# A hybrid decoder step on one core: where lower parts, a triangular substitution, merge weights and weight differences stand in the order of the engines

## The chip, the cores and the metric

The kernel runs on one core of a Trainium2 chip. Its time is the device time of one execution in microseconds (us), as the median of several runs. A profiled execution has a trace beside its time; the durations and waits below come from that one. The core's engines work beside each other, each on its own list of instructions in order: TensorE (PE in the profile, its weight loads PEld), VectorE (DVE), ScalarE (ACT) and GpSimd (POOL). SyncE (SP) issues most DMAs. An instruction whose inputs or output buffer are not ready holds back everything behind it on its engine.

## The reference, cut to what matters

One layer is computed for 1024 prompt tokens with 16 meta tokens ahead of them, and for 8 x 8 sample tokens, 1104 in all, of width 1024, in fp32.

```python
h = h + 0.5 * rms_norm(swiglu(rms_norm(h, g_pre), w_gate, w_up, w_down), g_post)     # 1024 -> 2816 -> 1024
qkv_pre, z, b, a, sq, sk, sv, g_dn, g_swa = split(rms_norm(h, mix_pre) @ w_in)
qkv = silu(causal_conv(qkv_pre))                                # 4 taps
o_dn, state = gated_delta(l2norm(q), l2norm(k), v, sigmoid(b), decay(a))     # chunks of 64; a unit lower
                                                                # triangular system per chunk and head
o_dn = rms_norm(o_dn) * silu(z)                                 # 8 heads, 128 x 128 states
o_sw = sink_softmax(windowed scores, ALiBi, 16 meta keys) @ v   # 8 query heads on 2 key heads
h = h + rms_norm((sigmoid(g_dn) * o_dn + sigmoid(g_swa) * o_sw) @ w_out, mix_post)
h = h + 0.5 * rms_norm(swiglu(rms_norm(h, g_pre2), ...), g_post2)
```

The new states and the windows of keys and values are outputs too.

## The kernel before

Every large product is made of three fp32r products: a value is split into an upper part (`wh`, `xh`: a cast on ScalarE) and a lower part (`wl`, `xl`: the value less its upper part, a subtraction), and upper x upper, upper x lower and lower x upper are summed in PSUM. So each slice of weights costs a DMA into `raw`, a cast and a subtraction before TensorE can use it.

Order: TensorE runs its instructions in the order of the program's text. On the other engines the framework's scheduler orders them by its own estimate of when each is ready; `keep_in_program_order(op)` pins an operation to the place that the text gives it, and `issue_after(ins)` puts what is issued inside behind `ins` on that instruction's engine. The text itself is woven: generators yield after each few matmuls, and `weave((steps, begin, end, count), ...)` mixes them in proportion. `steps_of(g, n)` takes n steps of one generator.

The stages in order, with the names that matter here:

- **First feed-forward** (0 to about 720 us). Gate ("g") and up ("u") products are made by a fast 2 x 2 block scheme of seven products for pairs of blocks of hidden columns. `gate_up` runs the products 1, 2, 6, 5, 7, 4, 3 into the PSUM banks A, B and C; `w_op` makes their weights from four raw quarters, for products 5, 6, 7 and 4 by differences `T` on VectorE (L256, L267), and `w_split` casts them (L281) and takes their lower parts on POOL (L282). After a product VectorE adds the bank into sums: `u2` after 6, `s` after 7 (L354), then the third sum `u3` = `s` + bank C (L357), after which C is free for product 3. `self.order[0]` is the first pair.
- **Mixer, start** (`before`, 730 to 810). While the feed-forward's last tiles pass through post-norm, residual and pre-norm (transposes L580 into one of two PSUM buffers `tr`, read by L626; L627 and L100 scale rows by factors `rp` and `rn`, whose Square is on ScalarE, L81, and whose power is on POOL, L82 and L83), the first projections of `w_in` already run in three rounds: `ba_steps` and the keys of heads 0 and 1. `w_in(col)` casts a slice on ScalarE (L764) and takes its lower part on POOL (L765); slices 8 and 9 are those keys' weights.
- **Keys, triangular systems, window attention** (810 to 1260). `lane_solve(size 64)` inverts the 128 triangular systems on VectorE in 62 steps of two operations, L1062 (`ltmp` = products) and L1064 (`la` += `ltmp`). They are issued by `solving(...)` one step per ten matmul steps of the query projections that run beside the window attention's blocks (32 blocks in four rounds p = 0 to 3 of eight; TensorE's rounds start at 1031.7, 1095.3, 1162.75 and 1230.85). A block: scores `sc` (L1217 on), VectorE adds the mask into `s` (L1220) and takes row maxima (L1189), ScalarE exponentials, transposes `pt`, casts `ptoh` (L1247), lower parts `ptol` (L1248), then `po` (L1257). The solved systems are stored to memory as they are and, by four ScalarE copies (L1094), transposed; the heads read them later. The pool of `la` gives its memory to the heads' convolution buffers in round 3.
- **Heads** (1260 to 1850). For each head `chain` carries the state through eight tiles: `ch` = R b (L1593), copy `xs` on ScalarE (L1595), `ch` = kd xs (L1598), new state S; `normed` makes the factor `f` on POOL (L1548) and `on` on ScalarE (L1549), `emit` transposes it (L1631). Beside it run the next head's projections and `z_gate`, which evaluates a gate piece by piece (`tz`, L1380). For the last head `z_gate` gets `done = mg.load_w`: after each of its three pieces the buffers of that piece of the mixer's input are free and take slices of `w_out`: DMA (L1709), casts in halves (L1712), lower parts on POOL (L1713).
- **Merge** (1835 to 1970). `begin` multiplies the first tile by `w_out` for heads 0 to 6 while the last chain ends, `begin_last` adds head 7 and copies the two banks out (L1765). The next tile's `yl` is split by L1729 and L1730, and TensorE goes on with `dn` (L128).
- **Second feed-forward** (1970 to 2685), as the first.

## Time and profile before

| | |
|---|---|
| median of 3 runs | 2686.57 us (2686.21 to 2691.09) |
| the profiled execution | 2687.11 us |
| its span, first to last instruction | 2685.2 us |
| mean granted TensorE clock | 0.991 |
| TensorE busy | 2604.9 us of the span |
| VectorE, ScalarE, POOL busy | 1556.6, 1127.4 and 1290.1 us |

The median describes the kernel; the profiled execution is the one that can be opened. TensorE's share of the span is so high that what matters is the list of its waits: each names the waiting line, the engine and line that released it, the sum, how often, and the longest. The granted clock in a table of stretches tells whether TensorE ran at full rate (1.00) or at half (0.50) there.

### The profile page before, as it was taken

To read this page: it belongs to the slowest core of one execution; us is meant where nothing else is said; L and a number is where in the kernel's file an instruction comes from. 1 tells how busy PE (TensorE), PEld (TensorE's weight loads), DVE (VectorE), ACT (ScalarE), POOL (GpSimd) and SP (SyncE) were. 2 spreads that over 40 slices of the span, in tenths; PEclk is the share of its full clock that TensorE was granted. 3 is DMA by queue.
4 is the path that set the end of the run, shared out by engine and by line. 5 is a ranking of instruction groups with operands and counts; after the bars stand their busy time and mean duration, and the time that the engine had idled before them with its cause. 6 is when DMAs were issued, how large, how long until landed. Compare 5 with 4: busy or idle time off the path is not lost. (4 is left out here: it accounts for less than half of the span.)

```text
span 2685.2 us, 49482 instructions
## 1 busy us (share of the span) xinstructions
PE 2604.9 (97%) x19053; PEld 2483.4 (92%) x19053; DVE 1556.6 (58%) x2295; ACT 1127.4 (42%) x2720; POOL 1290.1 (48%) x1223
## 2 busy tenths in 40 slices
PE   7999999999989998999999999998999999999998
PEld 7999999999988997888889999997789999999998
DVE  7656565545676669945454444443556656554566
ACT  6333343422145633566444444454443334334221
POOL 6656555445535733433343333344556555554471
PEclk9999999999999999999999999999999999999999
DMA  4343343667544753454333333334433434338764
GB/s 162 115 156 144 133 166 116 242 227 253 189 141 140 221 164 111 124 176 118 98 100 90 91 97 95 99 107 142 141 125 138 154 128 160 123 137 318 242 224 143
DMA packets 229568, 406.46 MB, mean 151 GB/s; under 512 B 59750, under 2 KB 121350, under 8 KB 229046
## 3 DMA queue, kind: packets, MB, share of 16 engines
q1 hardware_dynamic: 209030, 324.75, 37.2%
q10 hardware_dynamic: 20304, 78.56, 7.4%
q8 instruction: 150, 2.46, 0.4%
q14 instruction: 84, 0.69, 0.1%
HBM read 264.36 MB, written 140.53 MB: 151 GB/s over the span
## 5 line engine op out<-in xcount | busy, mean ns | idle before, releaser
L132 PE MATMUL gu<-xh,wl 128*128 128x512 f32 (+3 forms) x1456 | 495.4, 340 | 0.0
L128 PE MATMUL gu<-xh,wh 128*128 128x512 f32 (+3 forms) x1456 | 492.9, 339 | 0.0
L130 PE MATMUL gu<-xl,wh 128*128 128x512 f32 (+3 forms) x1456 | 492.2, 338 | 0.0
L282 POOL TENSOR_TENSOR wl<-T,wh 128x512 fp32r<-128x512 f32 x246 | 330.5, 1349 | 321.6 <-ACT wh L281 247.5
L492 PE MATMUL y<-hb,wh 128*128 128x256 f32 (+2 forms) x2528 | 430.5, 290 | 2.9 <-DVE acc L503 1.3
L282 POOL TENSOR_TENSOR wl<-raw,wh 128x512 fp32r<-128x512 f32 x200 | 282.8, 1422 | 254.3 <-ACT wh L281 193.3
L492 PEld LDWEIGHTS y<-hb,wh 128*128 128x128 f32 x2528 | 365.8, 188 | 4.3 <-DVE acc L503 1.8
L281 ACT CAST wh<-T 128x512 fp32r<-128x512 f32 x246 | 152.5, 620 | 368.7 <-PE B L316 115.5
L128 PEld LDWEIGHTS gu<-xh,wh 128*128 128x128 f32 x1456 | 278.0, 191 | 16.6 <-issue 0.9
L130 PEld LDWEIGHTS gu<-xl,wh 128*128 128x128 f32 x1456 | 278.0, 191 | 16.5 <-issue 0.4
L132 PEld LDWEIGHTS gu<-xh,wl 128*128 128x128 f32 x1456 | 278.0, 191 | 16.4 <-issue 0.4
L492 PE MATMUL y<-hb,wl 128*128 128x256 f32 (+2 forms) x1264 | 271.7, 288 | 0.2 <-POOL wl L282 0.2
L281 ACT CAST wh<-raw 128x512 fp32r<-128x512 f32 x200 | 122.3, 620 | 280.7 <-PE C L316 84.0
L503 DVE TENSOR_TENSOR acc<-acc,y 128x552 f32<-128x552 f32 (+4 forms) x216 | 144.9, 679 | 138.8 <-PE y L492 138.3
L765 POOL TENSOR_TENSOR wl<-raw,wh 128x1024 fp32r<-128x1024 f32 x60 | 145.5, 2425 | 159.9 <-ACT wh L764 130.4
L492 PEld LDWEIGHTS y<-hb,wl 128*128 128x128 f32 x1264 | 207.0, 188 | 0.5 <-POOL wl L282 0.5
L256 DVE TENSOR_TENSOR T<-raw,raw 128x512 f32<-128x512 f32 x124 | 119.9, 972 | 113.3 <-POOL wl L282 113.3
L1548 POOL TENSOR_TENSOR f<-f,mhalf 128x1 f32<-128x1 f32 (+1 forms) x72 | 54.5, 757 | 128.0 <-DVE f L1546 126.5
L267 DVE TENSOR_TENSOR T<-raw,T 128x512 f32<-128x512 f32 x62 | 64.5, 1042 | 65.1 <-POOL wl L282 64.7
L923 DVE SCALAR_TENSOR_TENSOR cv<-pc,cw,cv 128x1131 f32<-128x1131 f32 x48 | 66.8, 1393 | 31.0 <-POOL cv L920 30.7
L256 DVE TENSOR_TENSOR T<-raw,T 128x512 f32<-128x512 f32 x62 | 63.2, 1028 | 33.2 <-POOL wl L282 33.1
L1064 DVE TENSOR_TENSOR la<-la,ltmp 72x14 f32<-72x14 f32 (+37 forms) x76 | 75.3, 991 | 1.4
(592 smaller groups left out, 7304.8 us busy)
## 6 DMA issues: line engine op xcount, KB each, us to landing
hb<-hid SPq DMA_DIRECT2D x71, 552.0 KB
hb<-hid SPq DMA_DIRECT2D x71, 544.0 KB
hid<-hs ACTq DMA_DIRECT2D x69, 552.0 KB
hid<-hs ACTq DMA_DIRECT2D x69, 544.0 KB
raw<-in_w_in_dram SPq DMA_DIRECT2D x58, 512.0 KB
raw<-in_ffn_w_gate_dram SPq DMA_DIRECT2D x100, 256.0 KB
raw<-in_ffn_w_up_dram SPq DMA_DIRECT2D x94, 256.0 KB
raw<-in_ffn_w_down_dram SPq DMA_DIRECT2D x88, 256.0 KB
```

Source lines behind the costliest of these rows:

```text
L128: nc.tensor.matmul(ps, wh, xh, start=first and i == 0, stop=False)
L130: nc.tensor.matmul(ps, wh, xl, start=False, stop=False)
L132: nc.tensor.matmul(ps, wl, xh, start=False, stop=last and i == n - 1)
L256: pin(self.nc.vector.tensor_tensor(out=b[name], in0=b[x], in1=b[y], op=ALU.subtract))
L267: nc.vector.tensor_tensor(out=s, in0=b["21"], in1=s, op=ALU.subtract)
L281: self.nc.scalar.copy(hi, s)
L282: self.nc.gpsimd.tensor_tensor(out=lo, in0=s, in1=f32(hi), op=ALU.subtract)
L492: self.nc.tensor.matmul(self.view(ps[d], (i,)), w[x][:, d * P:(d + 1) * P], hb[:, y, lo:hi], start=j + x + y == 0, stop=j == len(items) - ...
L503: dve = lambda out, x, y: nc.vector.tensor_tensor(out=out, in0=x, in1=y, op=ALU.add)
L765: nc.gpsimd.tensor_tensor(out=lo, in0=raw, in1=f32(hi), op=ALU.subtract)
L923: nc.vector.scalar_tensor_tensor(out=cv, in0=pc[:, w:w + PADW], scalar=self.cw[:, j, w:w + 1], in1=cv, op0=ALU.mult, op1=ALU.add)
L1064: nc.vector.tensor_tensor(out=a[:n, 0:j, j + 1:size], in0=a[:n, 0:j, j + 1:size], in1=t, op=ALU.add)
```

## The change

Four edits, one to a stage.

1. `w_in` takes the engine of the lower part as an argument, and the keys' slices 8 and 9 take theirs on VectorE; slice 9 is issued after the first of the three rounds, behind a later Square. The rounds mix the three streams in another order, 80, 64 and 48 steps where it was 64 each.
2. In `lane_solve` the product of each of the 62 large steps is pinned to its place in the text.
3. `load_w` issues its DMAs at once and then yields after each half of a slice; the casts are pinned, `z_gate` takes one half every four of its steps from step 14 of the next piece on, and what is left of the last piece is woven beside `begin`. The two copies of L1765 go from ScalarE to VectorE.
4. In `gate_up` the weights of the first pair's up product 6, and the differences for them, are issued behind the gate's third sum.

The places where the order of the engines moves (line numbers of the changed kernel are larger, by 4 to 20; numbers after a name tell tiles apart). POOL in the mixer's start, before and then changed; `rp_8925` is the factor for the tile whose L627 the timeline shows at 766:

```order
L900 MEMSET pc_9124 128x3
L901 COPY pc_9124<-hist_8976 128x8x3
L765 TENSOR_TENSOR wl_9008<-raw_9003,wh_9007 128x1024
L82 TENSOR_SCALAR rp_8925<-rp_8925 128x1
L83 TENSOR_TENSOR rp_8925<-rp_8925,mhalf_64 128x1
L765 TENSOR_TENSOR wl_9012<-raw_9005,wh_9011 128x1024
L82 TENSOR_SCALAR rn_8933<-rn_8933 128x1
L83 TENSOR_TENSOR rn_8933<-rn_8933,mhalf_64 128x1
```

```order
L82 TENSOR_SCALAR rp_8925<-rp_8925 128x1
L83 TENSOR_TENSOR rp_8925<-rp_8925,mhalf_64 128x1
L907 MEMSET pc_9181 128x3
L908 COPY pc_9181<-hist_8976 128x8x3
L82 TENSOR_SCALAR rn_8933<-rn_8933 128x1
L83 TENSOR_TENSOR rn_8933<-rn_8933,mhalf_64 128x1
```

Both subtractions have left POOL; on VectorE `wl_9008` now stands ahead of L626 of that tile, and the other lower part between L626 and L627 of the next.

VectorE where the window's first scores arrive (`s_11772` is the first block's), before and then changed:

```order
L1141 TENSOR_TENSOR vtl_11194<-pt_11663,vth_11193 128x4x128
L1064 TENSOR_TENSOR la_11184<-la_11184,ltmp_11185 128x23x40
L1062 TENSOR_TENSOR ltmp_11185<-la_11184 128x936
L1064 TENSOR_TENSOR la_11184<-la_11184,ltmp_11185 128x24x39
L1062 TENSOR_TENSOR ltmp_11185<-la_11184 128x950
L1220 SCALAR_TENSOR_TENSOR s_11772<-scst_11202,sc_11774 128x144
L1220 SCALAR_TENSOR_TENSOR s_11772<-scst_11202,sc_11779 128x144
L1064 TENSOR_TENSOR la_11184<-la_11184,ltmp_11185 128x25x38
L1189 TENSOR_REDUCE nmb_11784<-s_11772 128x2
```

```order
L1149 TENSOR_TENSOR vtl_11194<-pt_11663,vth_11193 128x4x128
L1228 SCALAR_TENSOR_TENSOR s_11772<-scst_11202,sc_11774 128x144
L1228 SCALAR_TENSOR_TENSOR s_11772<-scst_11202,sc_11779 128x144
L1197 TENSOR_REDUCE nmb_11784<-s_11772 128x2
L1198 TENSOR_SCALAR nmb_11784<-nmb_11784 128x2
L1201 RECIPROCAL dnb_11785<-dnb_11785 128x2
L1174 CAST vm_11196<-fm_11746 48x256
L1175 TENSOR_TENSOR vm_11196<-fm_11746,vm_11196 16x256
```

All of the large substitution has moved behind the first block's scores. Of its 124 operations 49 stood ahead of the first scores, 36 in round 0 and 39 in round 1; now 41, 39 and 44 stand in rounds 0, 1 and 2.

ScalarE in the last head's chain, before and then changed (`xh_3953` holds four slices of `w_out`, `xs` is the chain's copy):

```order
L1380 ACTIVATE tz_21482<-gu_21415 128x512
L1712 CAST xh_3953_21485<-raw_21487 128x512 x2
L1712 CAST xh_3953_21485<-raw_21493 128x512 x2
L1712 CAST xh_3953_21485<-raw_21499 128x512 x2
L1595 COPY xs_21515<-ch_21513 128x128
```

```order
L1388 ACTIVATE tz_21482<-gu_21413 128x512
L1611 COPY xs_21499<-ch_21497 128x128
L1560 ACTIVATE sq_21515,so_21111<-o_21513 128x128
L1606 ACTIVATE qs_21532<-oq_21530,e_1440_9689 128x128
L1732 CAST xh_3953_21485<-raw_21487 128x512
L1565 ACTIVATE on_21469<-o_21513,f_21517 128x128
L1611 COPY xs_21550<-ch_21548 128x128
```

The six casts ahead of `xs` are now spread singly over the next three tiles. On VectorE in both feed-forwards the two sums that end in `u3g` (L354, L357) stand ahead of five `T` differences that stood between them and the first sum.

The diff:

```diff
@@ -325,7 +325,10 @@
         nc = self.nc
         st = self.st.setdefault((f, kind), {})
         for p in prods:
-            w = self.w_op(b, p, (f, kind, p)) if (p, "w") not in st else st[p, "w"]
+            with ExitStack() as behind:
+                if (p, kind, f) == (6, "u", self.order[0]):
+                    behind.enter_context(self.c.tc.issue_after(self.st[f, "g"]["third"]))
+                w = self.w_op(b, p, (f, kind, p)) if (p, "w") not in st else st[p, "w"]
             if len(parts) == 1:
                 st[p, "w"] = w
             bank = {1: a_bank, 2: a_bank, 6: "B", 7: "B", 4: "B", 5: "C", 3: "C"}[p]
@@ -354,7 +357,8 @@
                     nc.vector.tensor_tensor(out=st[out], in0=st[x], in1=ps, op=ALU.add)
                 if p == 7:
                     st["u3"] = self.v("u3" + kind)
-                    nc.vector.tensor_tensor(out=st["u3"], in0=st["s"], in1=self.view(st["C"], parts), op=ALU.add)
+                    st["third"] = nc.vector.tensor_tensor(out=st["u3"], in0=st["s"], in1=self.view(st["C"], parts),
+                                                          op=ALU.add).ins
             if len(parts) == 2 and p != 6:
                 next(self.late, None)
 
@@ -755,14 +759,15 @@
         queue.dma_start(raw, self.I["w_in"][col])
         return raw
 
-    def w_in(self, col, raw=None):
+    def w_in(self, col, raw=None, low=None):
 
         c, nc = self.c, self.nc
+        low = low or nc.gpsimd
         raw = raw or self.w_load(col, nc.sync)
         hi = c.t(self.wp, [P, KD, P], F32R, tag="wh")
         lo = c.t(self.wp, [P, KD, P], F32R, tag="wl")
         nc.scalar.copy(hi, raw)
-        nc.gpsimd.tensor_tensor(out=lo, in0=raw, in1=f32(hi), op=ALU.subtract)
+        low.tensor_tensor(out=lo, in0=raw, in1=f32(hi), op=ALU.subtract)
         return hi, lo
 
     def proj(self, *args, **kw):
@@ -802,13 +807,15 @@
         self.x = [{} for _ in range(H)]
         self.ba = self.c.t(self.pcp, [P, PADW + 3], tag="pc", bufs=3)
         raw = [self.w_load(8 + h, self.nc.scalar) for h in range(2)]
-        self.ready = {8: self.w_in(8, raw[0])}
-        tc = self.c.tc
-        with tc.issue_after(self.c.squares[-2]), tc.issue_after(self.c.factors[-2]):
-            self.ready[9] = self.w_in(9, raw[1])
+        self.ready = {8: self.w_in(8, raw[0], self.nc.vector)}
         first = self.ba_steps(), self.keys_conv(0, PIECES), self.keys_conv(1, PIECES)
-        for streams in rest:
-            weave((chained(*(steps_of(g, m) for g, m in zip(first, (16, 24, 24)))), 0, 1, 64), *streams)
+
+        for j, (order, streams) in enumerate(zip(((0, 1, 0, 1), (2, 2, 0), (1, 2)), rest)):
+            count = [(16, 24, 24)[i] for i in order]
+            weave((chained(*(steps_of(first[i], n) for i, n in zip(order, count))), 0, 1, sum(count)), *streams)
+            if not j:
+                with self.c.tc.issue_after(self.c.squares[-4]):
+                    self.ready[9] = self.w_in(9, raw[1], self.nc.vector)
         self.first = first
 
     def gates(self, tp):
@@ -1059,8 +1066,9 @@
         def step(j):
             w = size - 1 - j
             t = tmp[:n, 0:j * w].rearrange("p (r c) -> p r c", c=w)
-            nc.vector.tensor_tensor(out=t, in0=a[:n, 0:j, j:j + 1].to_broadcast([n, j, w]),
-                                    in1=a[:n, j:j + 1, j + 1:size].to_broadcast([n, j, w]), op=ALU.mult)
+            pin = self.c.tc.keep_in_program_order if size > 16 else lambda op: op
+            pin(nc.vector.tensor_tensor(out=t, in0=a[:n, 0:j, j:j + 1].to_broadcast([n, j, w]),
+                                    in1=a[:n, j:j + 1, j + 1:size].to_broadcast([n, j, w]), op=ALU.mult))
             nc.vector.tensor_tensor(out=a[:n, 0:j, j + 1:size], in0=a[:n, 0:j, j + 1:size], in1=t, op=ALU.add)
 
         return [lambda j=j: step(j) for j in range(1, size - 1)]
@@ -1384,10 +1392,18 @@
 
         if done:
             ws = self.w_in(24 + h), self.w_in(44 + h)
+            beside = iter(())
             for i in (2, 0, 1):
-                for w, first in zip(ws, (True, False)):
-                    yield from self.proj_piece(w, WHOLE[i], evac(first), 1088)
-                done(i)
+
+                for j, _ in enumerate(chained(*(self.proj_piece(w, WHOLE[i], evac(first), 1088)
+                                                for w, first in zip(ws, (True, False))))):
+                    if j >= 14 and j % 4 == 2:
+                        next(beside, None)
+                    yield
+                drain(beside)
+                beside = done(i)
+                next(beside)
+            self.left = beside
         else:
             yield from self.proj_steps(24 + h, evac(True), ntok=1088)
             yield from self.proj_steps(44 + h, evac(False), ntok=1088)
@@ -1671,7 +1687,7 @@
                 begin = mg.begin()
                 streams += [(steps_of(begin, 1), 0.6, 0.6, 1)]
             weave(*streams)
-        weave((begin, 0, 1, 42), (out, 0.1, 0.2, 1))
+        weave((begin, 0, 1, 42), (out, 0.1, 0.2, 1), (self.left, 0.15, 0.5, 4))
         drain(mg.begin_last(self.hd[H - 1]["Z"][:, 0:P]))
 
     def run(self, mg, es):
@@ -1702,16 +1718,20 @@
         c, nc = self.c, self.nc
         parts = new_chunk(c, self.xp[i], i)
         ks = ((2, 3, 4, 5), (6, 7), (0, 1))[i]
-        flat = [x.rearrange("p k t -> p (k t)") for x in parts]
+        flat, loaded = [x.rearrange("p k t -> p (k t)") for x in parts], []
         for j, k in enumerate(ks):
             wh, wl = (x[:, j * D:(j + 1) * D] for x in flat)
             raw = f32(c.t(self.m.wraw, [P, KD, P], F32R, tag="raw")).rearrange("p k f -> p (k f)")
             nc.sync.dma_start(raw, self.I["w_out"][:, k, :])
+            self.w[k] = wh, wl
+            loaded.append((raw, wh, wl))
+        yield
+        for raw, wh, wl in loaded:
             for q in range(2):
                 cols = slice(q * D // 2, (q + 1) * D // 2)
-                nc.scalar.copy(wh[:, cols], raw[:, cols])
+                c.tc.keep_in_program_order(nc.scalar.copy(wh[:, cols], raw[:, cols]))
                 nc.gpsimd.tensor_tensor(out=wl[:, cols], in0=raw[:, cols], in1=f32(wh[:, cols]), op=ALU.subtract)
-            self.w[k] = wh, wl
+                yield
 
     def pair(self, yh, yl):
 
@@ -1762,7 +1782,7 @@
             drain(self.mm(self.ps0[half], yh, yl, half, P, range(H - 1, H), False, True))
         self.o0 = f32(c.t(self.first, [P, H, P], F32R, tag="yh")).rearrange("p h t -> p (h t)")
         for half in range(2):
-            nc.scalar.copy(self.o0[:, half * 512:half * 512 + 512], self.ps0[half])
+            nc.vector.tensor_copy(self.o0[:, half * 512:half * 512 + 512], self.ps0[half])
         yield
 
     def finish(self, t, n, o, dump):
```

## The prediction

> **What bounds the kernel now.** I read the page first, then the waits of TensorE, then a table of stretches with the granted clock, then the timeline at each long wait. The page:
>
> ```profile
> span 2685.2 us, 49482 instructions
> PE 2604.9 (97%) x19053; PEld 2483.4 (92%) x19053; DVE 1556.6 (58%) x2295; ACT 1127.4 (42%) x2720; POOL 1290.1 (48%) x1223
> ```
>
> TensorE is busy for 97% of the span, so no edit that leaves its matmuls alone can win more than the 80 us in which it idles, plus what a lowered clock costs. The change leaves TensorE's instructions as they are (only the order of one short piece differs). It must therefore pay in single waits. In the waits of TensorE (line that waits, what released it, total us, times, longest), these five belong to the four parts of the change:
>
> ```profile
> PE ch L1598 <- ACT xs L1595: 6.3, 3, 2.9
> PE tr L580 <- DVE y L626: 5.7, 1, 5.7
> PE sc L1217 <- DVE s L1220: 4.5, 1, 4.5
> PE C L316 <- DVE u3g L357: 3.7, 2, 2.5
> PE po L1257 <- ACT ptoh L1247: 2.6, 1, 2.6
> ```
>
> They make 22.8 us. Behind most of them the clock is lowered. Stretches with busy times and granted clock (PEclk, 1.00 is full):
>
> ```profile
> core 0: us, PE busy (x) PEld busy (x) DVE busy (x) ACT busy (x) POOL busy (x), PEclk, DMA share, GB/s
> 773.48:780.30 6.82, 5.90 (x28) 5.93 (x29) 4.63 (x5) 2.43 (x5) 2.53 (x5) 0.50 0.65 230
> 1032.89:1036.30 3.41, 3.41 (x17) 3.41 (x16) 3.41 (x7) 1.47 (x6) 0.00 (x0) 0.50 0.17 45
> 1053.37:1056.78 3.41, 3.07 (x12) 2.91 (x13) 3.41 (x6) 1.53 (x4) 1.55 (x3) 0.50 0.30 86
> 1821.37:1824.78 3.41, 3.41 (x18) 3.41 (x18) 1.40 (x4) 0.86 (x3) 3.41 (x4) 0.50 0.64 186
> 1835.02:1838.43 3.41, 3.19 (x12) 2.90 (x13) 1.71 (x4) 0.57 (x4) 3.41 (x3) 0.50 0.07 19
> 78.73:82.14 3.41, 3.41 (x27) 3.41 (x28) 1.86 (x4) 2.02 (x4) 1.29 (x1) 1.00 0.15 53
> ```
>
> The last row, behind the wait at L316, stays at full clock. In the five others half of TensorE's busy time is lost: 2.95, 1.7, 1.5, 1.7 and 1.6 us, 9.5 in all.
>
> **Part 1, keys' lower parts (w_in on VectorE).** The wait at L580 in the timeline (start, duration, engine, line; in brackets the idle time and its releaser):
>
> ```profile
> 762.85 2.41 POOL L765 TENSOR_TENSOR wl<-raw,wh 128x1024 fp32r<-128x1024 f32 x1 [1.03 <-ACT wh L764]
> 766.01 2.39 POOL L765 TENSOR_TENSOR wl<-raw,wh 128x1024 fp32r<-128x1024 f32 x1
> 766.08 3.41 DVE L627 SCALAR_TENSOR_TENSOR y<-y,rp,res 128x1024 f32<-128x1024 f32 x1 [0.81 <-POOL rp L83]
> 771.84 1.28 DVE L100 SCALAR_TENSOR_TENSOR acc<-y,rn,g_mix_norm_pre 128x1024 f32<-128x1024 f32 x1
> 774.40 0.45 PE L580 MATMUL tr<-ident,acc 128*128 128x128 f32 x1 [5.74 <-DVE y L626]
> ```
>
> The first wl holds POOL, so tile 4's factor comes 0.81 us late; the second runs beside L627, which takes 3.41 us where L100, an operation of the same form, takes 1.28. Both wl leave POOL. L627 then starts at 765.27 and ends near 766.55 instead of 769.49, and the chain behind it shifts by 2.9 us; the new order of the matmuls puts another 0.9 us of projection ahead of the waiting transpose. The wait goes from 5.74 to about 1.9, the clock should hold (2.95). The cost: two wl on VectorE. No row shows a 128x1024 subtraction there; the 128x512 T rows below give 2 x 0.68 = 1.4 us alone and 2 x 1.76 = 3.5 beside POOL. I take 1.4, since POOL now has only factors there. The first lies in VectorE's wait for the Square ahead of L626 and costs nothing (if that hole is gone, 1.4); the second stands ahead of tile 5's L627, and I charge 1.2 for it in later waits for tr. 3.8 + 2.95 - 1.2 = 5.5; ends 2.5 (clock drops all the same) and 7.
>
> **Part 2, the pinned substitution.** Groups of VectorE from 979 to 1140 and one of ScalarE from 1138 to 1162, one instruction at the wait, and the four stretches between the rounds' starts:
>
> ```profile
> L1064 DVE TENSOR_TENSOR la<-la,ltmp 128x62 f32<-128x62 f32 (+31 forms) x63 | 72.5, 1151 | 1.0
> L1062 DVE TENSOR_TENSOR ltmp<-la 128x62 f32<-128x62 f32 (+31 forms) x63 | 56.5, 897 | 1.2
> L1094 ACT COPY ltmp<-la 128x1024 f32<-128x1024 f32 x4 | 8.2, 2049 | 4.6 <-DMA lrt_d<-ltmp 3.2 <-DVE la L1064 1.4
> 1027.04 3.17 DVE L1064 TENSOR_TENSOR la<-la,ltmp 128x936 f32<-128x936 f32 x1
> 979.00:1031.70 52.70, 48.59 (x298) 44.08 (x296) 51.05 (x55) 13.21 (x27) 15.83 (x8) 1.00 0.27 90
> 1031.70:1095.30 63.60, 58.90 (x366) 53.91 (x367) 61.90 (x95) 31.30 (x93) 23.30 (x30) 0.95 0.39 116
> 1095.30:1162.75 67.45, 65.92 (x436) 60.19 (x435) 51.96 (x103) 42.02 (x109) 26.31 (x36) 1.00 0.53 174
> 1162.75:1230.85 68.10, 68.10 (x489) 61.33 (x488) 28.53 (x71) 38.87 (x117) 19.55 (x30) 1.00 0.44 131
> ```
>
> Before, the substitution fills VectorE ahead of the first scores (51.05 of 52.70; the 3.17 us instruction stood ahead of their s) and in the first round (61.90 of 63.60), and is done by 1140. By the order of before, 49 of its 124 operations stand ahead of round 0, 36 in it and 39 in round 1; now none stands ahead, and 41, 39 and 44 stand in rounds 0, 1 and 2.
> - Ahead of round 0 the 4.47 us wait goes, and 1.7 of clock: +6.2.
> - Round 0 idles 63.60 - 58.90 = 4.7 us, the 2.6 at L1257 among it. It now holds the first 41 operations, many narrow: 22 us of other work (61.90 less 36 at the mean 1.1) and 41 at 0.8 make 55 of 63.6. I count 80% of the idle time, 3.8, and nothing for the 1.5 of clock.
> - Round 1 now holds operations 42 to 80, nearly the 50 to 85 that round 0 held. I price it as round 0 was, 4.7 of idle time where its own was 67.45 - 65.92 = 1.5: -3.2. VectorE is all but the bound there.
> - Round 2: 28.53 and 44 at 0.8 are 64 of 68.1, just hidden. What is late next is its end: ACT's four copies of la, 8.2 us, and the stores on SP fall into its last 30 us, ahead of the last block's casts, and POOL's memset of a buffer in the same memory waits for the last store. I charge 1.5 (0 to 5).
>
> Sum 6.2 + 3.8 - 3.2 - 1.5 = 5.3; ends -4 (all three rounds idle 4.7, with their clock) and 10.
>
> **Part 3, merge weights in steps.** The first of the two long waits at L1598, then the merge's start:
>
> ```profile
> 1817.57 3.21 ACT L1712 CAST xh<-raw 128x512 fp32r<-128x512 f32 x6
> 1820.67 0.26 ACT L1595 COPY xs<-ch 128x128 f32<-128x128 f32 x1
> 1820.99 0.49 PE L1598 MATMUL ch<-xs,kd 128*128 128x128 f32 x2 [2.86 <-ACT xs L1595]
> 1832.86 2.16 ACT L1712 CAST xh<-raw 128x512 fp32r<-128x512 f32 x4
> 1835.24 0.80 PE L1598 MATMUL ch<-xs,kd 128*128 128x128 f32 x2 [2.69 <-ACT xs L1595]
> 1850.64 1.07 ACT L1765 COPY yh<-gu 128x512 f32<-128x512 f32 x2 [9.95 <-PE gu L130]
> 1852.61 0.50 PE L128 MATMUL dn<-xh,yh 128*128 128x512 f32 x1 [1.77 <-ACT yh L1729]
> ```
>
> Six casts, then four, stand in one piece ahead of the copy xs that the state's chain needs. In the new order at most one half of a slice stands straight ahead of an xs, about 0.5 us (3.21 / 6). Both waits go, 2.86 + 2.69 = 5.5, and their clock, 3.3. Against it, three xs now have a cast or a tz right ahead: -1.2. The lower parts on POOL come singly, so the factors f and what waits on them lose some queueing: I give 0.8 (0 to 1.5). At 1850.64 the two copies leave ACT; yl's cast no longer stands behind them, but its subtraction now stands behind them on VectorE, so of 1.77 only 0.6 is won. The last slices come later on POOL; their matmuls stand past the chain's end, and I count no wait (up to 3 if one is late). 5.5 + 3.3 - 1.2 + 0.8 + 0.6 = 9.0; ends 4 and 10.5.
>
> **Part 4, third sum ahead of the second kind's differences.**
>
> ```profile
> 72.97 0.62 ACT L281 CAST wh<-T 128x512 fp32r<-128x512 f32 x1 [0.88 <-PE B L316]
> 73.75 1.76 DVE L267 TENSOR_TENSOR T<-raw,T 128x512 f32<-128x512 f32 x1 [1.18 <-POOL wl L282]
> 77.11 0.72 DVE L354 TENSOR_TENSOR sg<-u2g,B 128x552 f32<-128x552 f32 x1
> 77.86 0.73 DVE L357 TENSOR_TENSOR u3g<-sg,C 128x552 f32<-128x552 f32 x1
> 78.51 0.68 DVE L256 TENSOR_TENSOR T<-raw,T 128x512 f32<-128x512 f32 x1
> 78.73 0.36 PE L316 MATMUL C<-x30h,wh 128*128 128x256 f32 x1 [2.50 <-DVE u3g L357]
> ```
>
> The cast at 72.97 is released by product 7's last matmul on bank B, so B is complete there; TensorE wants C at 76.23. With the sums first, u3g ends near 74.5 and 2.50 goes; in the second feed-forward the other 1.2 of L316's 3.7. The differences follow from 74.5; the first pair takes 1.4 us, cast and lower part some 2.3 more, so the up-weights stand at 78.2, and TensorE wants them at 79.4, after the product on C. Worth 3.7; ends 1.5 (weights late by 2) and 3.9.
>
> **Sum.** 5.5 + 5.3 + 9.0 + 3.7 = 23.5. The profiled execution took 2687.11, so 2663.6; the median of the runs shown, 2686.57, is 0.5 lower, which gives 2663.1, or 2663. Faster or slower by under 0.2%, 5.4 us, is about what a measurement of this kernel cannot tell from no change.
>
> **The clock rule.** Stretches at half clock begin behind waits of 2.6 to 2.9 us in the rows above, and behind 2.50 at L316 not. [...]
>
> **Rivals.**
> - VectorE binds in rounds 1 and 2, and part 2 wins nothing: for it speaks that 61.90 of 63.60 left TensorE idle for 4.7; against it that nothing stands ahead of the first scores now. 23.5 - 5.3 = 18.2, or 14 at part 2's lower end: 2668 to 2673.
> - The pinned casts hold xs as before: ACT runs in order, and a cast that waits for a late slice blocks the copy behind it. For it: three buffers only; against: the first slices lie loaded 10 us early. Part 3 is then worth 1: 2671.
> - The half clock stays behind waits that only shrink (part 1's 1.9, part 3's small ones): 23.5 less 2.95 and 3.3, 2669.
> - Slower: every score, row maximum and ptol of the 24 blocks of rounds 0 to 2 queues behind one pinned operation of about 1.0 us. Three such per block are 72. Once 23.5 / 72 = 0.33 us of each reaches TensorE, the gain is gone; at 0.6 the time is 2706. Round 0 before had this crowding and lost 4.7 on 24 of them, 0.2 each, so it is unlikely.
> - The time saved is given back at transfers of the following stages: no change, 2684. Against it, no wait of TensorE for a transfer is among the long ones.
>
> **Chances.** [...] The first five are faster by over 5.4 us: 0.91; same 0.05; slower 0.04. The likeliest: 2663. Parts 1, 2 and 3 at their better ends, 7, 10 and 10.5, would make 2655; the upper end takes in the VectorE rival with part 3 a few us short: 2677.
>
> **What would show it.** Wait L580 at about 2; no L1217 wait over 1 us near 1027; half-clock stretches gone behind L1598; L316 waits for u3g gone; L1062 and L1064 spread to 1211; round 1 some 69 to 71 us long with VectorE over 95% busy. Wrong it would be if round 1 or 2 grows by over 6 us, or if a wait for ACT's casts stands where L1598's stood.

## The result, and the profile after

| | before | changed |
|---|---|---|
| median of 4 runs each, taken together | 2688.66 us | 2673.96 us (2667.11 to 2676.72) |
| ratio, with its 95% interval | | 0.9942 [0.9919, 0.9964] |
| the profiled execution, and its span | 2687.11, 2685.2 us | 2667.11, 2665.3 us |
| mean granted clock there | 0.991 | 0.994 |

A second measurement of the changed kernel, 6 runs, gave 0.9941 [0.9929, 0.9953]. The gain is 15 to 16 us; 23.5 were forecast. The two profiled executions lie 20.0 apart: the changed kernel's happened to be its fastest of four, with the highest clock, so single traces are read below together with those of the experiments.

The page after, busy times of the engines:

```profile
span 2665.3 us, 49487 instructions
PE 2601.2 (98%) x19053; PEld 2478.5 (93%) x19053; DVE 1547.3 (58%) x2299; ACT 1125.8 (42%) x2718; POOL 1293.5 (49%) x1221
```

The work is the same; 19.9 us of the span went, 3.7 of them from TensorE's busy time, the rest from its idle time. TensorE's waits after, those of the stages that the change touches (lines have moved by 4 to 20):

```profile
PE po L1265 <- DVE ptpl L1256: 3.9, 4, 1.3
PE sc L1300 <- POOL qp L1290: 2.0, 1, 2.0
PE dn L128 <- ACT yh L1749: 2.0, 1, 2.0
PE tr L584 <- DVE y L630: 1.6, 1, 1.6
```

The waits at L1217 for VectorE's s (4.5 us) and at L316 for u3g (3.7) have no row any more. L580, now L584, went from 5.7 to 1.6, and L1598, now L1614, from 6.3 to 1.4, its longest wait from 2.9 to 0.8. Against that, the waits for VectorE's ptpl inside the window's blocks, two of 1.1 in all before, are four of 3.9; the one for POOL's qp, early in round 3, is new; and the one for yh in the merge stayed (1.8 before).

To see where the time went, each trace was cut at the same matmuls, counted from the first, and the stretches compared. The rounds are cut where the prediction has them: at the first matmul from 1031.7, 1095.3, 1162.75 and 1230.85 on in the kernel before. All traces of the experiments are used, parted by whether the kernel has the part of the change that works in the stretch. Means in us, with the lowest and highest in brackets:

| stretch | without the part | with it | won | forecast |
|---|---|---|---|---|
| mixer's start and the stretch behind it (part 1) | 301.6 (300.9-303.0), 4 traces | 297.3 (296.7-298.1), 10 | 4.3 | 5.5 |
| last wait ahead of round 0 (part 2) | 6.3 (6.0-6.4), 5 traces | 1.8, 4 | 4.6 | 10.0, with the next row |
| round 0 | 63.8 (63.3-64.8), 5 | 55.2 (54.8-56.2), 4 | 8.6 | |
| round 1 | 67.5 (67.4-67.7), 5 | 71.3 (71.1-71.4), 4 | -3.7 | -3.2 |
| round 2 | 68.1, 5 | 71.4, 4 | -3.3 | 0 |
| start of round 3, 258 matmuls | 38.4 (37.5-40.4), 5 | 40.3 (40.0-40.5), 4 | -1.9 | -1.5, as round 2's end |
| last head's chain (part 3) | 34.5 (32.9-35.1), 4 | 27.2 (26.9-28.0), 10 | 7.3 | 8.4 |
| merge's start | 40.0 (39.2-40.8), 4 | 40.3 (39.4-41.0), 10 | -0.3 | 0.6 |
| first feed-forward's first pair (part 4) | 108.3 (107.2-109.3), 4 | 104.4 (103.4-105.5), 10 | 3.9 | 2.5 |
| second feed-forward's first pair | 46.4, 4 | 45.0, 10 | 1.4 | 1.2 |

Here part 2's rows use, with the part, only kernels with part 2 as the change has it. They sum to 4.3 for part 2 and to 20.9 for all four. Rounds 0, 1 and 2 in the trace of the changed kernel, and then round 2 cut where the substitution ends (columns as in the prediction's tables of stretches, where the rounds of before stand, cut within 0.4 us of these):

```profile
1019.35:1074.26 54.91, 54.74 (x368) 50.81 (x367) 46.94 (x93) 28.63 (x85) 20.91 (x27) 1.00 0.42 127
1074.26:1145.63 71.37, 66.64 (x436) 60.43 (x435) 70.76 (x104) 35.09 (x106) 30.46 (x30) 1.00 0.36 109
1145.63:1217.05 71.42, 68.75 (x490) 61.23 (x488) 59.06 (x114) 42.33 (x118) 25.22 (x33) 1.00 0.53 171
1145.63:1197.60 51.97, 49.30 (x348) 43.63 (x347) 51.03 (x95) 26.97 (x86) 19.76 (x23) 1.00 0.42 123
1197.60:1217.05 19.45, 19.45 (x144) 17.59 (x142) 8.02 (x20) 15.36 (x33) 5.46 (x10) 1.00 0.85 298
```

The wait of 4.5 us ahead of round 0 is gone, and in round 0 TensorE idles for 0.2 us instead of 4.7, with no half clock left there. In round 1 its idle time went from 1.5 to 4.7, with VectorE busy for 70.76 of 71.37 us. In round 2 it went from nothing to 2.7, and all of that lies ahead of 1197.6, where VectorE is busy for 51.03 of 51.97 us. Behind it, with ScalarE's copies running, TensorE does not idle.

Some expectations below were written with stretches cut elsewhere: what they call round 2's end (39.8 us before, 43.1 changed) is the last third of round 2 with the start of round 3.

### The profile page after: what moved, and what is told of

The parts are those of the page before. It is cut to its first block, busy times and chain, and to the rows that moved or that the text cites. A ratio compares the mean times of both kernels' runs of the same rounds, so it can differ in the third digit from the quotient of the medians.

```text
span 2665.3 us, 49487 instructions
## 1 busy us (share of the span) xinstructions
PE 2601.2 (98%) x19053; PEld 2478.5 (93%) x19053; DVE 1547.3 (58%) x2299; ACT 1125.8 (42%) x2718; POOL 1293.5 (49%) x1221
## 5 line engine op out<-in xcount | busy, mean ns | idle before, releaser
L770 POOL TENSOR_TENSOR wl<-raw,wh 128x1024 fp32r<-128x1024 f32 x58 | 139.7, 2409 | 162.0 <-ACT wh L769 132.4
L769 ACT CAST wh<-raw 128x1024 fp32r<-128x1024 f32 x60 | 62.9, 1048 | 32.8 <-PE gu L130 32.8
```

The lines of the kernel that those rows point to most:

```text
L770: low.tensor_tensor(out=lo, in0=raw, in1=f32(hi), op=ALU.subtract)
```

## The experiments

Ratios are to the kernel before on the same chip, with 95% intervals. Every kernel had 4 to 12 runs. The differences of under 0.2% between variants of the change are inside the intervals; there the stretches of the traces are what can be read, and they are of one execution each.

**Each part alone.** Four kernels: before, with the hunks of one part of the diff and no other. Part 1:

> The kernel before with part 1 alone (keys' lower parts on VectorE). By the offsets between the traces the mixer's start took 102.3 us before and 98.2 or 96.7 in two traces of the change. Theory: 3 to 6 us faster than before, 0.998 to 0.9989, the wait at the tr transposes down from 5.7 to under 2 us. Rival (the second wl on VectorE gives it back at the later tiles): under 2 us.

Part 2:

> The kernel before with part 2 alone (the pinned substitution). Traces of before and of the change show TensorE some 13 us earlier at the end of round 0 and only about 3 us earlier behind round 3's start, by the offset between the same matmuls. Theory A (won ahead of and in round 0, given back in rounds 1 and 2): this kernel is 2 to 5 us faster than before, 0.998 to 0.9993. Rival B (the giving back came from the other three parts' shift, not from the substitution): 10 to 13 us faster, 0.995.

Part 3:

> The kernel before with part 3 alone (merge weights in steps). By the offsets between the traces of before and of the change part 3 won 8.4 us up to the merge's start and lost 1.7 there. Theory: 6 to 8 us faster than before, ratio 0.997 to 0.9978. Rival (the forecast's 9.0 and no loss at the merge): 9 us, 0.9967.

Part 4:

> The kernel before with part 4 alone (third sum ahead of the second kind's differences). Both waits at L316 for u3g, 2.50 and 1.20 us, go; no half clock hung on them. Theory: 3.5 to 4 us faster, 0.9986. Rival (weights of up product 6 come late): a wait at B L316 for POOL's wl in their place, under 2 us gained.

| part alone | ratio | us, from the median of before beside it |
|---|---|---|
| 1 | 0.9987 [0.9976, 0.9998] | 3.5 |
| 2 | 0.9986 [0.9977, 0.9995] | 3.8 |
| 3 | 0.9979 [0.9971, 0.9988] | 5.6 |
| 4 | 0.9983 [0.9972, 0.9995] | 4.6 |

Each part wins by itself, and the four sum to 17.5, against 15 to 16 for the change; no interval excludes that they simply add. Parts 1 and 2 came out as expected, part 3 just short of the 6 to 8 us, part 4 above its 3.5 to 4. In the part 1 kernel the wait shrank just as in the change:

```profile
PE tr L580 <- DVE y L626: 1.6, 1, 1.6
```

**The change without part 2.** In `lane_solve` the product is issued unpinned:

```diff
-            pin(nc.vector.tensor_tensor(out=t, ..., op=ALU.mult))
+            nc.vector.tensor_tensor(out=t, ..., op=ALU.mult)
```

> The change without part 2 (parts 1, 3 and 4). Theory A: 14 to 17 us faster than before (the profiled run of the change was 20 faster, of which part 2 is 3), ratio 0.9937 to 0.9948; so close to the change that part 2 can hardly be told. Rival B: only 5 to 9 us faster, 0.997, since part 2 would carry 10 or more.

0.9944 [0.9930, 0.9958], against 0.9942 and 0.9941 for the change: the runs do not tell it from the whole change. Its trace shows the same exchange as the table: the last wait ahead of round 0 and round 0 are back at 6.4 and 63.3, round 1 at 67.7, round 2 at 68.1. Its start of round 3 took 40.4, so not every late start there is due to part 2.

**The change again.**

> The changed kernel once more, as the measure for the runs beside it. Its four runs went from 2667 to 2677 with granted clocks of 0.994 down to 0.990. Theory (which short waits halve the clock is left to chance): the runs again spread by 6 to 10 us, in step with the clock by 2 to 3 us per 0.001, around 0.9935 to 0.995 of before. Rival (the spread comes from transfers): no tie between clock and time.

0.9941 [0.9929, 0.9953]. The profiled span is 2670.7 where the first was 2665.3, of the same instructions. Its mean granted clock is 0.992, the first trace's 0.994. Its stretches at half clock (0.50), without the one in which the kernel ends, sum to 34.1 us where the first trace has 23.9 (and that of before 41.0). An estimate from these: half of the 10.2 is 5.1 of the 5.4.

**Substitution started earlier.** The cadence of the solver beside the stretch ahead of round 0, from one step in six to one in two:

```diff
-            weave((solving(self.q1, 0, 6), 0, 1, 72), (left, 0.15, 0.95, 3))
+            weave((solving(self.q1, 0, 2), 0, 1, 72), (left, 0.15, 0.95, 3))
```

> The change with the substitution's steps issued every 2 instead of every 6 matmul steps beside the first query projection: 14 of the 124 large operations stand ahead of round 0's scores, and 44, 40 and 26 in rounds 0 to 2 instead of 41, 39 and 44, so the substitution, its copies and its stores end some 10 us earlier in round 2. Theory A1 (the loss in round 2 is the late end: copies and stores meet the last blocks): 3 to 6 us faster than the change. Theory A2 (the loss is VectorE's crowding while the substitution runs): 0 to 2 us faster, since rounds 0 and 1 are as full as before. Rival C (operations ahead of the scores bring the old 4.5 us wait back): 3 or more us slower than the change.

0.9934 [0.9920, 0.9947]: no clear difference to the change. The operations ahead of round 0 and in rounds 0 to 2 went from 0, 41, 39, 44 to 14, 44, 40, 26. Round 1, and round 2 in two pieces, cut near the substitution's end:

```profile
1081.55:1149.14 67.59, 65.83 (x437) 60.26 (x435) 67.04 (x103) 33.61 (x102) 30.64 (x29) 1.00 0.38 114
1149.14:1176.90 27.76, 26.34 (x179) 22.70 (x177) 26.71 (x57) 15.81 (x49) 12.82 (x15) 1.00 0.44 127
1176.90:1220.91 44.01, 43.21 (x314) 38.77 (x312) 17.00 (x44) 31.42 (x78) 11.41 (x22) 1.00 0.66 217
```

Round 1 took 67.6 us, as in the kernel before (67.5), with VectorE busy for 67.04 of it; in the change it took 71.4 with 70.76. So a full VectorE does not by itself set what a round loses. Why one full round lost 3.7 us and the other nothing, no run here separates. Round 2 took 71.8: 2.1 more than the same matmuls before in the piece with VectorE full, and 1.6 more in the piece beside the four copies. The start of round 3 took 38.1, 2.4 less than in the change, and round 1 3.8 less, but round 0 took 60.0 where the change has 54.9. What was won late was thus lost early.

**Without the four copies.** The transposed solution is not made; the plain one is stored in its place, so the kernel leaves out that transposition:

```diff
-                at = tmp.rearrange("p (r c) -> p r c", c=64)
-                nc.scalar.copy(at, a[:, :, 16 * q:16 * q + 16].rearrange("p r c -> p c r"))
-                nc.sync.dma_start(out[:, 16 * q:16 * q + 16, :], at)
+                nc.sync.dma_start(out[:, 16 * q:16 * q + 16, :], a[:, 16 * q:16 * q + 16, :])
```

> The change without ScalarE's four copies of the solved systems: what should be stored transposed is stored as it is, straight from la, so the transposition is left out. Theory A1 (copies and the stores waiting for them disturb round 2's end): 3 to 5 us faster than the change, and the waits at the score matmul of the sample block and at the last casts shrink. Theory A2 (crowding of VectorE): within 1.5 us of the change.

0.9913 [0.9898, 0.9928]. The start of round 3 in the change and without the copies, and the one wait for qp that is left there:

```profile
1217.05:1257.51 40.46, 37.40 (x260) 31.80 (x259) 25.40 (x59) 27.23 (x89) 15.62 (x33) 0.96 0.49 136
1219.66:1256.25 36.59, 35.38 (x260) 30.56 (x259) 24.18 (x58) 24.63 (x86) 15.32 (x29) 1.00 0.51 143
```

```profile
PE sc L1298 <- POOL qp L1288: 0.9, 1, 0.9
```

36.6, against 40.5 with the copies: the copies at the end of the substitution are what made the start of round 3 late. Round 2 took 71.4 with and without them, and round 1 stayed long, 73.0, with a mean granted clock of 0.98 from 1117.7 to 1194.6, so the copies have no part in what these two lost. By the ratios, 0.9913 against 0.9942, the kernel is some 8 us faster than the change, twice what the trace shows at this place and more than the 3 to 5 that were expected; where the rest lies is open. In the changed kernel the timeline shows how they act (start, duration, engine, line; idle time and releaser in brackets):

```profile
1216.62 2.02 ACT L1102 COPY ltmp<-la 128x1024 f32<-128x1024 f32 x1 [0.81 <-DMA lrt_d<-ltmp]
1218.91 1.05 ACT L769 CAST wh<-raw 128x1024 fp32r<-128x1024 f32 x1
1220.04 2.36 POOL L770 TENSOR_TENSOR wl<-raw,wh 128x1024 fp32r<-128x1024 f32 x1 [3.69 <-ACT wh L769]
1222.34 0.77 POOL L1290 COPY qp<-q 128x64 f32<-128x64 f32 x4
1223.16 0.63 PE L1300 MATMUL sc<-kc,qp 128*32 128x152 f32 x8 [1.97 <-POOL qp L1290]
```

The fourth copy waits for a store, a weight's cast waits behind it, POOL's lower part waits for the cast, and qp, which needs none of them, stands behind the lower part.

**The copies on VectorE.**

```diff
-                nc.scalar.copy(at, a[:, :, 16 * q:16 * q + 16].rearrange("p r c -> p c r"))
+                nc.vector.tensor_copy(at, a[:, :, 16 * q:16 * q + 16].rearrange("p r c -> p c r"))
```

> The change with the four transposing copies of the solved systems on VectorE, which stands idle for 1 to 4 us at a time behind the substitution's end, instead of ScalarE. Leaving the copies out had been 6 to 8 us faster than the change by the ratios. Theory A1 (2.05 us each on ScalarE in front of casts and exponentials is what hurts round 2's end): 2 to 6 us faster than the change. Rival (the stores' place on the queue of SP hurts): within 1.5 us of the change, as the stores stay.

0.9929 [0.9917, 0.9941]. The wait for qp went, but another took its place, for the load of kc:

```profile
PE sc L1300 <- DMA kc<-in_kcT_dram: 2.3, 1, 2.3
```

The start of round 3 took 39.5, 0.9 less than in the change. The theory was then that the four stores, which wait for their copies on SP's queue, hold back the load of kc behind them.

**Their stores on ScalarE's queue too.**

```diff
-                nc.sync.dma_start(out[:, 16 * q:16 * q + 16, :], at)
+                nc.scalar.dma_start(out[:, 16 * q:16 * q + 16, :], at)
```

> The change with the four transposing copies on VectorE and their four stores issued by ScalarE instead of SP. With the copies on VectorE alone the stretch that holds round 2's end took 42.3 us against 43.1 in the change and 39.4 without copies, and the sample block's score waited 2.3 us for kc, a load that stands behind the last store on SP. Theory (the stores on SP's queue hold kc back): that wait goes, the stretch takes 39.5 to 40.5, 2 to 3 us faster than with the copies on VectorE alone. Rival (the transfers themselves are slow there): the wait stays near 2 us.

0.9923 [0.9908, 0.9938], the lowest ratio of the kernels that compute everything, though its interval overlaps that of the change. The wait for kc is still there, and the start of round 3 took 39.2:

```profile
PE sc L1300 <- DMA kc<-in_kcT_dram: 1.9, 1, 1.9
```

So the theory of SP's queue fell. What holds kc back is open. The share of busy DMA engines in that stretch does not tell the kernels apart: 0.49 in the change, 0.51 without the copies, and neither has a wait for kc.

**Both together, copies and stores moved and the substitution earlier.**

> The same with the substitution's steps issued three times as densely beside the first query projection (14 of 124 operations ahead of round 0, 30 instead of 44 left for round 2 with the copies among them). Earlier it took 2 us off round 2, 2.9 off its end, and put 3.4 on the first round. Theory: no faster than the kernel beside it, within 2 us, since the end's loss is already gone. Rival (less VectorE crowding in round 2 counts): 3 us faster.

0.9946 [0.9930, 0.9961]: no faster than the change, and by the medians 6.7 us slower than the kernel beside it without the earlier start, where within 2 us was expected. Round 1 took 67.6 again and the start of round 3 38.6, but round 0 took 62.2, so what one edit gave the other took. The two do not add.

**The merge.** In `load_w` the lower parts of the slices that come second go to VectorE:

```diff
-                nc.gpsimd.tensor_tensor(out=wl[:, cols], ..., op=ALU.subtract)
+                (nc.vector if i == 1 else nc.gpsimd).tensor_tensor(out=wl[:, cols], ..., op=ALU.subtract)
```

> The change with the last two slices' lower parts of the merge weights on VectorE instead of POOL. In the trace of the change POOL's last addition to Z stands behind four of them (1827.0), so the store and the load of yl come late and TensorE waits 1.96 us at dn. Theory: the addition runs some 3 us earlier, the wait at dn and its half-clock stretch go, 2 to 4 us faster than the change. Rival (the two copies of the banks on VectorE hold yl's subtraction back): the wait at dn goes from 1.96 to about 1.5 only, 0 to 1 us faster.

0.9943 [0.9931, 0.9955]: no gain. The reason for it was this row of places in the changed kernel:

```profile
1825.74 1.30 POOL L1733 TENSOR_TENSOR xl<-raw,xh 128x512 fp32r<-128x512 f32 x1
1827.00 1.29 POOL L1654 TENSOR_TENSOR Z<-Z,yw 128x512 f32<-128x512 f32 x1
1828.32 0.32 SPq L1655 DMA_DIRECT2D y_d<-Z  x1
1828.69 2.26 SPq L1827 DMA_DIRECT2D yl<-y_d  x2
1832.29 0.94 ACT L1749 CAST yh<-yl 128x896 fp32r<-128x896 f32 x1 [7.22 <-DMA yl<-y_d]
1833.28 0.50 PE L128 MATMUL dn<-xh,yh 128*128 128x512 f32 x1 [1.96 <-ACT yh L1749]
```

POOL adds the last Z behind the lower parts; Z is stored, loaded again as yl, cast, and only then does TensorE go on. With those lower parts on VectorE the addition waited for its own load instead, and the wait of 1.96 turned into two:

```profile
1828.39 1.81 POOL L1654 TENSOR_TENSOR Z<-Z,yw 128x512 f32<-128x512 f32 x1 [1.69 <-DMA yw<-yw_d]
```

```profile
PE dn L132 <- DVE yl L1750: 0.8, 1, 0.8
PE dn L128 <- DVE yh L1785: 0.6, 1, 0.6
```

That is 1.4 instead of 2.0, near the 1.5 of the rival, and both are for VectorE now, the second for a bank copy that the change moved there. But the two waits of 0.6 and 0.8 are also there with part 3 alone and with the copies on VectorE, where the lower parts are all on POOL. So the 2.0, found in both traces of the change, isn't set by the place of these lower parts alone, and the theory that they hold up the merge fell.

## Why the prediction was right, and where it was off

The direction and the range (2655 to 2677) held; the time came out 11 above 2663, to which the sum as worked, at a chance of 0.53, had led. Some 4 of the 11 come from the start of the sum: it went from 2686.57, while the 55 runs of the kernel before in the experiments have a mean of 2690.3. The profiled execution of before was among its faster ones. Most of the rest is that less was won. The ratios on one chip put the gain at 15 to 16 us; the mean of 10 runs of the changed kernel is 2673.1, 17.2 below that of the 55, over all chips. So 6 to 8 us less were won than forecast. Of these, 2.6 come from the terms, 23.5 against 20.9. The stretches that no part touches were some 1 us longer in three traces with the whole change than in the five of before and of single parts; within either group the traces differ by 4 to 8 us there. The rest is not located.

**Part 1: right, 4.3 for 5.5.** The wait fell to 1.65 as forecast (1.9). What the trace shows of the step on VectorE:

```profile
758.94 1.23 DVE L770 TENSOR_TENSOR wl<-raw,wh 128x1024 fp32r<-128x1024 f32 x1 [0.20 <-ACT wh L769]
761.50 1.28 DVE L631 SCALAR_TENSOR_TENSOR y<-y,rp,res 128x1024 f32<-128x1024 f32 x1
768.09 1.06 PE L584 MATMUL tr<-ident,acc 128*128 128x128 f32 x8 [1.65 <-DVE y L630]
```

The lower part takes 1.23 (1.4 was taken), and L631, the L627 of before, is down from 3.41 to 1.28 with no subtraction of POOL beside it. The mis-sized term is the clock, "the clock should hold (2.95)": behind the wait the first trace has full clock (1.00 from 769.35 to 772.76), but in the second trace of the same kernel a lowered clock (0.55) stands behind the same wait of 1.6 (its row at 770.10 is in the last section). The rival of a clock that stays was true in one of these two executions.

**Part 2: 4.3 for 5.3, by larger terms on both sides.** Ahead of round 0 and in it 13.2 were won where 10.0 were counted; among them is the clock behind the wait at L1257 (0.50 from 1053.37 before, 1.00 over the whole of round 0 after), for which "nothing" was counted. Round 1 came out as priced: "4.7 of idle time where its own was" 1.5 is what the trace shows, and 3.7 us of time for 3.2. That price was partly luck, since with the earlier start a round 1 just as full lost nothing. The failed term is round 2, "64 of 68.1, just hidden": it lost 3.3 us. The sum over the round was near (59.06 of 71.42), but the substitution is not spread over it: it fills VectorE for the first 52 us, and there TensorE idled the 2.7. The end's "1.5 (0 to 5)" was 1.9, and the mechanism was as told in kind (ScalarE's copies and the casts behind them), but early in round 3 and by way of POOL's qp. The sum thus lies between the forecast and the rival "VectorE binds in rounds 1 and 2", which had part 2 at nothing: rounds 1 and 2 came out that way, but what was won ahead of them stayed. That the net came within 1 us is in part luck, as errors of 3.2 and 3.3 cancelled.

**Part 3: 7.0 for 9.0.** The two waits behind six and four casts went, as the chain in the changed kernel shows, with a single cast ahead of the second xs:

```profile
1806.64 0.27 ACT L1611 COPY xs<-ch 128x128 f32<-128x128 f32 x1
1807.10 0.38 PE L1614 MATMUL ch<-xs,kd 128*128 128x128 f32 x2
1809.11 0.61 ACT L1732 CAST xh<-raw 128x512 fp32r<-128x512 f32 x1
1809.62 0.40 ACT L1565 ACTIVATE on<-o,f 128x128 f32<-128x128 f32 x1
1810.05 0.27 ACT L1611 COPY xs<-ch 128x128 f32<-128x128 f32 x1
1810.39 0.47 PE L1614 MATMUL ch<-xs,kd 128*128 128x128 f32 x2
```

No wait of TensorE stands at either copy. The chain's stretch won 7.3, with 8.4 to be had from the waits, their clock, the casts and "0.8" for POOL. The failed term, about as large, is the merge: "of 1.77 only 0.6 is won" became a mean loss of 0.3, as the waits at its start went from 2.2 in all (1.8 and 0.4) to 1.4 to 2.3, and in the trace of the change a stretch of half clock lies there (0.50 from 1834.31 to 1837.72), where that of before has full clock (1.00 from 1838.43 to 1957.90). Some of the clock that was won in the chain thus came back there in this trace. The rival that pinned casts hold xs did not come about.

**Part 4: 5.3 for 3.7, the one term that was too small.** The sum is early enough that C is free:

```profile
72.50 0.73 DVE L357 TENSOR_TENSOR sg<-u2g,B 128x552 f32<-128x552 f32 x1 [5.11 <-PE B L316]
73.27 0.73 DVE L360 TENSOR_TENSOR u3g<-sg,C 128x552 f32<-128x552 f32 x1
75.35 0.28 PE L316 MATMUL C<-x30h,wh 128*128 128x256 f32 x1
```

u3g ends at 74.0 (74.5 was forecast), TensorE takes C at 75.35 with no wait. What was left out is the clock behind the removed wait, since the row of before stood at full clock. Two of the four traces without part 4 have it lowered there: with part 1 alone and with part 3 alone. The waits there of the kernels with part 1, 3 and 2 alone, and the stretch behind each in the same order:

```profile
PE C L316 <- DVE u3g L357: 2.2, 1, 2.2
PE C L316 <- DVE u3g L357: 2.9, 1, 2.9
PE C L316 <- DVE u3g L357: 2.5, 1, 2.5
```

```profile
81.30:84.70 3.40, 3.40 (x19) 3.40 (x19) 1.18 (x2) 0.62 (x1) 0.72 (x2) 0.58 0.25 80
77.50:80.90 3.40, 3.20 (x14) 3.23 (x15) 1.99 (x4) 1.84 (x3) 1.29 (x1) 0.50 0.17 61
78.70:82.10 3.40, 3.40 (x28) 3.40 (x28) 1.85 (x4) 2.00 (x4) 1.29 (x1) 1.00 0.10 34
```

Behind 2.2 and 2.9 the clock is lowered (0.58 and 0.50), behind 2.5 it is full (1.00). So the wait cost more in the mean than in the one trace that was read.

**The clock.** The prediction's sum held 7.95 us of clock. Over all runs the mean granted clock rose from 0.9898 (55 runs) to 0.9923 (10). An estimate: 0.0025 of 2680 us is 6.7 us, some 0.4 of the 17.2 gained. So clock was won, but on average and not behind each wait (0.55 at 770.10 in the second trace).

**What was to show it.** L584 at 1.65, no wait for s at the first scores, the half clock gone behind L1598's two waits (granted clock 1.00 from 1226.73 to 1834.31) and the waits for u3g gone: all four as told. Round 1 was to be "69 to 71 us long with VectorE over 95% busy": it took 71.4 in this trace, with VectorE busy for 99% of it. Rounds 1 and 2 grew by 3.7 and 3.3, well under the 6 that would have made the account wrong. The substitution ended at 1197.6, not at 1211.

## What to carry to other kernels

A long operation that is moved from in front of a wait into busy rounds must be priced where it will stand, not over the round: round 2 had room for it in the sum (59.06 of 71.42), yet TensorE idled 2.7 us in the part that it filled. Nor has a full engine one price: round 1 lost 3.7 us in one order and nothing in another, with VectorE 99% busy in both. The end of a moved chain moves too; follow what comes behind its last step (here four copies, then a cast, a lower part and qp) over all engines before the end is called cheap. Where the traces show a lowered clock behind a wait in some executions (here 0.58, 0.50 and 1.00 behind the same wait in three kernels), count it as a part of the wait's cost in the mean, compare several traces, and start the sum from a mean of many runs rather than from the profiled one.

## What the runs showed of the hardware that was not expected

The length of a wait did not tell what clock followed it. One program, two traces: in the first the waits of 1.65 at 766, of 1.42 at 1288 and of 1.01 at 1342 are followed by full clock (1.00), in the second by a lowered one (0.55, 0.55 and 0.53 over the stretches from 770.10, 1292.30 and 1347.0). In each of the traces of before and of the change the stretches of half clock begin whole multiples of 3.413 us apart (773.48, 811.02 and 855.40 before; 1223.32, 1834.31 and 1940.12 changed). Cut at such multiples, the 3.41 us that hold the end of these waits (with smaller waits beside them), in the first trace:

```profile
765.94:769.35 3.41, 1.76 (x16) 1.36 (x13) 3.41 (x4) 1.67 (x3) 1.42 (x2) 1.00 0.18 73
1288.18:1291.59 3.41, 1.94 (x14) 1.41 (x12) 0.62 (x3) 3.17 (x15) 0.00 (x0) 1.00 0.79 251
1342.79:1346.20 3.41, 2.59 (x17) 2.16 (x17) 1.68 (x7) 3.41 (x13) 0.89 (x3) 1.00 0.07 14
```

The same in the second, some 0.4 later, while the wait of 1.42 ends 0.2 earlier (1289.75 for 1289.94), and then the stretches behind the first two there, with the lowered clock:

```profile
766.32:769.74 3.42, 1.56 (x13) 1.29 (x14) 3.42 (x5) 1.14 (x3) 0.95 (x2) 1.00 0.05 18
1288.56:1291.97 3.41, 1.60 (x11) 1.34 (x11) 1.19 (x5) 3.35 (x15) 0.00 (x0) 1.00 0.76 229
1343.18:1346.59 3.41, 1.91 (x13) 1.64 (x14) 1.98 (x5) 3.41 (x16) 0.88 (x3) 1.00 0.07 14
770.10:773.50 3.40, 3.40 (x19) 3.23 (x18) 1.21 (x2) 2.41 (x5) 0.92 (x3) 0.55 0.94 308
1292.30:1295.70 3.40, 3.40 (x12) 2.99 (x13) 0.55 (x2) 1.66 (x4) 0.80 (x1) 0.55 0.15 37
```

TensorE idles for 1.65, 1.47 and 0.82 us of the first three, and for 1.86, 1.81 and 1.50 of the next three. The traces of before and of the change have 15 stretches of half clock (0.50) from 60 us on, the end aside. Of the 3.41 us ahead of each, TensorE idles for 1.35 to 3.42 us in 13, and for none in two (from 807.61 before and from 800.07 changed). But full clock followed 1.65 and 1.47 us in the rows above, and in the trace of before 1.57 of the 3.41 us from 77.16 and 1.82 of those from 790.54. So in these traces neither the length of a wait nor the idle time in such a piece tells by itself which clock comes next; what decides it was not shown.

The spread of the runs goes with the clock: the changed kernel's first four runs went from 2667.11 at a mean clock of 0.994 to 2676.72 at 0.990.
